# Exponentials in one piece, priorities for the weights' splits and the last scan, and gate tiles per group, in a Mamba-2 plus differential attention trunk

## The chip, the cores and the metric

The kernel runs on one core of a Trainium2 chip. The metric is the device time of one launch in microseconds (us); for several runs the median is given. The engines are named as in the profile: PE is TensorE (matrix products and transposes), PEld its loading of weights, DVE is VectorE, ACT is ScalarE, POOL is GpSimd, SP is SyncE, which issues the DMA transfers here.

## The reference, cut to what matters

One sequence of 512 tokens with 1024 features passes two layers and a last RMSNorm, all in float32.

```
mamba2_layer:  h = rms_norm(x);  z, xbc, dt = split(h @ w_in)
               xbc = silu(causal_conv4(xbc));  xs, B, C = split(xbc)
               per group g (8), heads r (4), head dim 64, state 128:
                 acs   = cumsum(a * dt)                      # inside a chunk
                 y     = (C B^T * exp(acs_l - acs_s), causal) @ (xs*dt)
                       + (C @ state) * exp(acs)
                 state = state*exp(acs_end) + B^T (xs*dt*exp(acs_end - acs))
               y = group_rms_norm((y + d_skip*xs) * silu(z));  x = x + y @ w_out
shared_kv:     k, v = split(rms_norm(x) @ w_kv)
diff_attention_layer: two softmax maps per head on k, weights A1 - lambda*A2, @ v,
               per-head norm, silu gate;  x = x + (...) @ w_out
out = rms_norm(x)
```

The change touches only the first layer: the decays `exp(acs_l - acs_s)`, the gate `silu(z)`, the preparation of the weights, and the order in which the last group's scan is worked.

## The kernel before, in words

**Products in two parts.** Each large product is computed from operands that are split in a high and a low part of a reduced float32 format: `a*b` becomes `ah*bh + ah*bl + al*bh`, three matmuls (`mm3`). A weight segment of 128x2048 is loaded into a `raw` tile (two buffers) by one DMA of SP, then **split** in four (later eight) pieces: `head` makes the high part `whi` on ACT (a scaled copy), `rest` the low part `wlo` on DVE (`raw*gain - whi`). `whi` and `wlo` have two buffers each, so a segment's split waits until the segment two before it has been used by TensorE. `load` (line 122) issues the DMA and gives back the pieces, `lay` (169) writes a piece's two instructions, `fetch` (174) does both for all segments up to a number, and `use` (179) calls it for the next two segments whenever a segment is taken.

**The first layer.** Its work is two streams. The dense one, `stream_a` (521), is all products with weights, in the order `z0 g0 g1 z1 g2 g3 z2 g4 o0 g5 z3 g6 g7 o1 o2 o3`: `z` projects the gates of two groups (four tiles of 128 tokens by 512, PSUM tiles `pz`), `g` projects one group's B, C and x (PSUM tiles `pg`, then the convolution on DVE and ACT), and `o` is the out-projection of two groups (PSUM tiles `po`, added into `x_tok` on DVE). Each `z`, `g` and `o` takes two segments. All of them share four PSUM banks ("mm"). The other stream is `ssd(g)` (552), the scan of a group. It works through C B^T (`pcb`), transposes of B and x (`pbt`, `pxt`), the product with the decays on DVE (`dec` times `pcb`), the states (`psA`, `psB`, `hst`), the output inside the chunk (`pyd`) and from the state (`po` from `hst`), the gate (`u` times `zt`, line 626), the group norm (squares on ACT, the root on DVE, the scaled copy `tmp` on ACT), and the transposes `pyt`, of which `yh` and `yl` are made for the out-projection. The scans use three PSUM banks of their own ("ss") and mostly one SBUF buffer for each kind of tile. The text of the program asks for a group's scan as soon as the group's projection is written.

**Decays.** `decays(j)` (532) prepares two groups. For each it loads the cumulated logarithms, spread over all partitions (a 1 MB DMA into `dec`, two buffers), copies the chunk ends into `een` on POOL, subtracts the tokens' own value and masks, head by head, on POOL. Then for each group ACT takes the exponential of `een` (128x8) and of `dec` in two halves of 128x1024. `een` scales the states in the scan (lines 590 and 594). It is called at the beginning for groups 0 and 1 and within the scan of each odd group for the next two.

**Gates.** `z_out` (344) takes Silu of a 128x512 tile of `pz` on ACT into a `zs` tile (six buffers). Such a tile holds both groups of a pair; it comes free when the later one's scan has used it.

**What sets the order.** Up to line 687 the program is only a list with dependencies. When it is compiled, a scheduler plays it on a model of the engines: among the instructions of an engine that are ready at that moment of the play it takes the one of the highest priority, which is the place in the text where nothing else is said, and gives out the tiles' buffers in the same order. What comes out is a fixed order for each engine; on the chip each engine works through its own list, and an instruction that has to wait holds all behind it on that engine. From line 687 on the order of DVE, ACT and TensorE is that of the text, with the splits placed by hand (`paced`, `use_b`). The loads of ACT's function tables are put in after the scheduling, wherever the next function needs another table.

## Time and profile before

| | |
|---|---|
| median of 3 runs | 737.57 us (736.57 to 738.35) |
| the profiled execution | 736.51 us |
| its span, first to last instruction | 734.7 us |
| granted TensorE clock, mean | 0.998 |
| DMA | 70.83 MB, mean 96 GB/s |

A row of a timeline gives the start in the span, the duration, the engine, the line, the operation, the tile written and the tiles read, the size, and the number of instructions merged in the row; in brackets stands how long the engine had been idle before it and what released it. A row of the waits gives who waited for whom, the sum in us, how often, and the longest. A row of the groups gives the count, the busy time, the mean of one in ns, and the idle time before. Most rows bear line 53, since a helper there records the operations of DVE, ACT and PE; they are told apart by their tiles. A matmul's record is longer than the time after which the next one starts.

### The profile page before, as it was taken

Reading aid. Unit: us, or ns where it says so; the run is one execution under the profiler, and the core shown is the slowest. Engines: PE = TensorE matmul, PEld = TensorE weight load, DVE = VectorE, ACT = ScalarE, POOL = GpSimd, SP = SyncE. Lnnn points to the kernel's source line nnn. Section 1 sums busy time; section 2 is a strip of 40 time slices with the busy share of each in tenths; the row PEclk is TensorE's granted clock in tenths of the full one; section 3 lists DMA queues with packets and bytes.
Section 4 is the critical chain, followed back from the end, with each engine's and each line's share of the span. In section 5 each row is a group of like instructions: output and inputs, shape, how many; then the busy total and the mean of one; then the engine's idle time right before and its main releaser. Section 6 shows DMA issues by size and latency. Waiting matters only on the chain.

```text
span 734.7 us, 10327 instructions
## 1 busy us (share of the span) xinstructions
PE 723.1 (98%) x3733; PEld 605.0 (82%) x3733; DVE 530.8 (72%) x1202; ACT 445.3 (61%) x975; POOL 114.8 (16%) x158
## 2 busy tenths in 40 slices
PE   9999999999999999999999999999999999999996
PEld 7788878888887888877888879888898898889874
DVE  5679955798568669469895655666757857785886
ACT  6849672864829356256433258766766766766566
POOL 0117231402233141150110201000000000000002
PEclk9999999999999999999999999999999999999999
DMA  8552313224132233132113220331221131122003
GB/s 314 215 193 97 128 45 116 78 95 172 59 114 65 108 115 116 58 116 102 71 58 114 87 86 8 115 115 58 65 109 57 58 116 58 58 80 93 29 1 114
DMA packets 12914, 70.83 MB, mean 96 GB/s; under 512 B 1728, under 2 KB 2496, under 8 KB 5312
## 3 DMA queue, kind: packets, MB, share of 16 engines
q1 hardware_dynamic: 12576, 69.90, 26.5%
q8 instruction: 29, 0.48, 0.3%
q10 hardware_dynamic: 288, 0.28, 0.1%
q14 instruction: 21, 0.17, 0.1%
HBM read 68.02 MB, written 2.16 MB: 96 GB/s over the span
## 4 chain that ended last, share of the span: by engine, by line
PE 86%; DVE 6%; ACT 5%; issue 1%; DMA 1%; POOL 0%; ACTq 0%; POOLq 0%; SPq 0%
PE pg L53 20%; PE po L53 13%; PE pz L53 10%; PE pt L53 7%; PE pv L53 6%; PE pq L53 6%; PE pk L53 6%; PE pyd L53 4%; PE pb L53 3%; PE sc L53 3%; PE pc L53 2%; DVE wlo L53 2%; ACT L53 1%; PE pyt L53 1%; PE pxt L53 1%
## 5 line engine op out<-in xcount | busy, mean ns | idle before, releaser
L53 DVE SCALAR_TENSOR_TENSOR wlo<-raw,prm,whi 128x512 fp32r<-128x512 f32 (+1 forms) x256 | 151.4, 640 | 49.6 <-ACT whi L53 49.2
L53 ACT ACTIVATE whi<-raw,prm 128x512 fp32r<-128x512 f32 (+1 forms) x256 | 137.1, 609 | 58.5 <-PE pz L53 12.4
L53 PE MATMUL pg<-a_hi,whi 128*128 128x512 f32 x256 | 102.4, 401 | 0.4 <-DVE xc L53 0.4
L53 PE MATMUL pg<-a_hi,wlo 128*128 128x512 f32 x256 | 102.7, 404 | 0.0
L53 PE MATMUL pg<-a_lo,whi 128*128 128x512 f32 x256 | 101.4, 397 | 0.0
L53 DVE SCALAR_TENSOR_TENSOR xc<-pg,prc,xc 128x511 f32<-128x511 f32 (+2 forms) x96 | 70.0, 743 | 4.4 <-ACT xc L53 3.6
L53 PEld LDWEIGHTS pg<-a_hi,whi 128*128 128x128 f32 x256 | 48.2, 188 | 11.4 <-issue 0.8
L53 PEld LDWEIGHTS pg<-a_hi,wlo 128*128 128x128 f32 x256 | 48.1, 188 | 11.0
L53 PEld LDWEIGHTS pg<-a_lo,whi 128*128 128x128 f32 x256 | 48.2, 188 | 10.8
L53 PE MATMUL po<-whi,yh 128*128 128x512 f32 x128 | 50.9, 400 | 0.7 <-ACT yh L53 0.6
L53 PE MATMUL po<-wlo,yh 128*128 128x512 f32 x128 | 50.9, 400 | 0.4 <-DVE wlo L53 0.4
L53 PE MATMUL pz<-wlo,a_hi 128*128 128x512 f32 x128 | 50.5, 401 | 0.0
L53 PE MATMUL pz<-whi,a_lo 128*128 128x512 f32 x128 | 50.1, 399 | 0.0
L53 PE MATMUL po<-whi,yl 128*128 128x512 f32 x128 | 49.9, 396 | 0.0
L53 PE MATMUL pz<-whi,a_hi 128*128 128x512 f32 x128 | 49.6, 400 | 0.0
L53 ACT ACT_TABLE_LOAD x33 | 42.3, 1283 | 9.5 <-DVE xc L53 7.9
L957 POOL TENSOR_TENSOR ot<-ot,fg 128x512 f32<-128x512 f32 x4 | 5.1, 1285 | 257.6 <-PE pc L53 256.4
L53 ACT ACTIVATE s<-s,mx 128x128 f32<-128x128 f32 (+3 forms) x64 | 35.6, 559 | 9.5 <-DVE mx L53 9.3
L580 POOL TENSOR_TENSOR xe<-xdt,tok 128x256 f32<-128x256 f32 x24 | 15.4, 672 | 152.5 <-DVE xdt L53 152.5
L53 DVE CUSTOM_DVE_ANT_0 s<-sc,bias 128x128 f32<-128x128 f32 (+3 forms) x64 | 29.4, 488 | 12.3 <-PE sc L53 11.9
L53 PE MATMUL pv<-whi,b_hi 128*128 128x256 f32 x128 | 36.6, 286 | 0.0
L53 ACT ACTIVATE tmp<-dx 128x256 f32<-128x256 f32 x32 | 13.1, 411 | 38.0 <-DVE dx L53 38.0
(244 smaller groups left out, 1749.1 us busy)
## 6 DMA issues: line engine op xcount, KB each, us to landing
raw<-in_w_in SPq DMA_DIRECT2D x23, 1024.0 KB, 4.9
raw<-in_w_kvqg SPq DMA_DIRECT2D x16, 1024.0 KB, 4.8
dec<-acs_d SPq DMA_DIRECT2D x8, 1024.0 KB, 4.8
raw<-in_w_out SPq DMA_DIRECT2D x8, 1024.0 KB, 4.7
raw<-in_w_bo SPq DMA_DIRECT2D x4, 1024.0 KB, 4.8
x_tok<-in_x SPq DMA_DIRECT2D x4, 512.0 KB, 9.4
out<-ot SPq DMA_DIRECT2D x7, 256.0 KB, 2.4
raw<-in_w_in SPq DMA_DIRECT2D x4, 256.0 KB, 5.4
```

The source lines that it names most:

```text
L53: i = op(*args, **kw)
L580: GP.tensor_tensor(out=xe[:, c], in0=xdt[:, c], in1=toe_tok[:, c, hs].unsqueeze(2).to_broadcast([P, R, HD]), op=ALU.mult)
L957: GP.tensor_tensor(out=o, in0=o, in1=f, op=ALU.mult)
```

## The change

- `decays` is given the groups' numbers; for each group `dec` and `een` are now two parts of one tile of 2056 columns, and one Exp takes the whole tile. The DMA, the copy and POOL's work stay. All exponentials of a pair still come behind both groups' POOL work in the text.
- `fetch` writes the pieces of a split under high priority (the DMA is issued at the normal one). This holds for the segments that `fetch` loads, those of the first layer.
- The last group's scan, `ssd(7)`, is written under high priority.
- `z_out` makes two Silu of 128x256 into tiles of their own (twelve buffers), one for each group.
- The split of the one segment that borrows the buffers of `dec` takes the first 2048 columns of the larger tile.

```
 def fetch(upto):
     while fetched[0] < min(upto, len(segs)):
-        for piece in load(fetched[0])():
-            lay(piece)
+        pieces_ = load(fetched[0])()
+        with tc.high_priority():
+            for piece in pieces_:
+                lay(piece)
...
 def z_out(j, t, ps):
-    zs = bp2.tile([P, 512], F32, tag="zs", name=f"zs{j}_{t}", bufs=6)
-    A.activation(zs, ps, AF.Silu, scale=r_col[:, t:t + 1])
-    zt[j, t] = zs
+    for i in range(2):
+        zs = bp2.tile([P, 256], F32, tag="zs", name=f"zs{j}_{t}_{i}", bufs=12)
+        A.activation(zs, ps[:, i * 256:(i + 1) * 256], AF.Silu, scale=r_col[:, t:t + 1])
+        zt[2 * j + i, t] = zs
...
-def decays(j):
-    for g in (2 * j, 2 * j + 1):
+def decays(gs):
+    for g in gs:
         hs = slice(R * g, R * g + R)
-        dec = bp.tile([P, R, NQ, P], F32, tag="dec", name=f"dec{g}", bufs=2)
+        both = bp.tile([P, N_DEC], F32, tag="dec", name=f"dec{g}", bufs=2)
+        dec = both[:, 0:R * NQ * P].rearrange("p (h c l) -> p h c l", h=R, c=NQ)
+        een = both[:, R * NQ * P:].rearrange("p (h q) -> p h q", h=R)
...
-        een = small.tile([P, R, 2], F32, tag="een", name=f"een{g}")
         GP.tensor_copy(een, dec[:, :, 1:3, P - 1])
...
-    for g in (2 * j, 2 * j + 1):
-        dec, een = decs[g]
-        A.activation(een, een, AF.Exp)
-        for h in range(0, R, 2):
-            A.activation(dec[:, h:h + 2], dec[:, h:h + 2], AF.Exp)
+    for g in gs:
+        A.activation(decs[g][2], decs[g][2], AF.Exp)
...
-            V.tensor_tensor(out=u[:, c], in0=u[:, c], in1=zt[g // 2, c][:, zo:zo + 256], op=ALU.mult)
+            V.tensor_tensor(out=u[:, c], in0=u[:, c], in1=zt[g, c], op=ALU.mult)
...
-        ssd(g)
+        if g < G - 1:
+            ssd(g)
+        else:
+            with tc.high_priority():
+                ssd(g)
```

## The prediction

> **What bounds the kernel now.** I read the page first, then the list of waits of TensorE, then the timelines around each of those waits. The page's busy table:

> ```profile
> span 734.7 us, 10327 instructions
> PE 723.1 (98%) x3733; PEld 605.0 (82%) x3733; DVE 530.8 (72%) x1202; ACT 445.3 (61%) x975; POOL 114.8 (16%) x158
> ```

> TensorE is busy for 98% of the span; no other engine is near it. A change that touches no matmul, as this one, can gain only what TensorE stands still. The list of TensorE's waits, without the one at the very start and two at the very end, is short:

> ```profile
> PE pyt L53 <- ACT tmp L53: 1.0, 2, 0.7
> PE po L53 <- ACT yh L53: 0.6, 1, 0.6
> PE po L53 <- DVE wlo L53: 0.4, 1, 0.4
> PE pg L53 <- DVE xc L53: 0.4, 1, 0.4
> ```

> All of these lie in the first part (the Mamba layer, up to about 450 us), the only part that the change touches. They add up to 2.4 us of 734.7. The timeline of TensorE shows where they are and what they really cost:

> ```profile
> 227.69 0.71 PE L53 MATMUL po<-whi,yh 128*128 128x512 f32 x2
> 228.82 0.50 PE L53 MATMUL po<-wlo,yh 128*128 128x512 f32 x1 [0.42 <-DVE wlo L53]
> ...
> 236.38 0.40 PE L53 MATMUL po<-wlo,yh 128*128 128x512 f32 x1
> 236.62 0.40 PE L53 MATMUL po<-whi,yl 128*128 128x512 f32 x1
> 237.67 0.44 PE L53 MATMUL pyt<-ident,tmp 128*128 128x128 f32 x2 [0.65 <-ACT tmp L53]
> ...
> 337.50 0.40 PE L53 MATMUL pg<-a_hi,wlo 128*128 128x512 f32 x1
> 338.31 0.47 PE L53 MATMUL pg<-a_hi,whi 128*128 128x512 f32 x1 [0.41 <-DVE xc L53]
> ...
> 428.10 0.39 PE L53 MATMUL po<-whi,yl 128*128 128x512 f32 x1
> 428.88 1.64 PE L53 MATMUL pyt<-ident,tmp 128*128 128x128 f32 x8 [0.39 <-ACT tmp L53]
> 431.08 0.50 PE L53 MATMUL po<-whi,yh 128*128 128x512 f32 x1 [0.57 <-ACT yh L53]
> ```

> A matmul's record lasts 0.40 us, but the next starts 0.24 us after it (236.38 to 236.62), so the printed idle time hides some 0.16 us: a wait costs its printed time and about 0.16 us of refilling. The five are then worth 0.42+0.16 = 0.58 (weights' low part late, 228.8), 0.81 (the scan's output late on ACT, 237.7), 0.57 (a PSUM bank freed late, 338.3), 0.55 and 0.73 (both before and behind the last scan's transposes, 428.9 and 431.1). The sum is **3.24 us, the most that can be won**; below that stands TensorE's own work.

> **The exponential in one instruction.** Now each group has three Exp activations: the small een as soon as it is copied, and two halves of dec. The scheduler places them apart, among Silu activations that need another table. Around the second stall ACT did this:

> ```profile
> 220.03 1.28 ACT L53 ACT_TABLE_LOAD   x1
> 221.32 0.21 ACT L53 ACTIVATE een<-een 128x8 f32<-128x8 f32 x1
> 221.55 1.28 ACT L53 ACT_TABLE_LOAD   x1
> ...
> 224.85 2.56 ACT L53 ACTIVATE whi<-raw,prm 128x512 fp32r<-128x512 f32 x4
> 227.42 1.28 ACT L53 ACT_TABLE_LOAD   x1
> 228.72 1.06 ACT L53 ACTIVATE dec<-dec 128x1024 f32<-128x1024 f32 x1
> 229.80 1.28 ACT L53 ACT_TABLE_LOAD   x1
> ...
> 232.97 1.28 ACT L53 ACT_TABLE_LOAD   x1
> 234.26 1.06 ACT L53 ACTIVATE dec<-dec 128x1024 f32<-128x1024 f32 x1
> ...
> 237.12 1.70 ACT L53 ACTIVATE tmp<-dx,y_y 128x256 f32<-128x256 f32 x4
> ```

> Five loads, 6.4 us, in 14 us, ahead of the tmp that TensorE waited for at 237.67. One exponential per group needs at most one load before and one behind, so three of these five go: 3 x 1.28 = 3.84 us less ACT ahead of tmp, against a wait of 0.65. The een's 0.21 goes too.

> ```profile
> L53 ACT ACT_TABLE_LOAD x33 | 42.3, 1283 | 9.5 <-DVE xc L53 7.9 <-PEq L1112 1.2
> ```

> Over the kernel I expect 20 to 26 loads instead of 33, 9 to 17 us less of ACT's 445. Elsewhere TensorE's list names ACT only at the last scan, so that is worth nothing there. [...]

> Waiting for the whole of dec instead of half costs the scan nothing, since dec is made far ahead of its use. For the last group, the two halves on ACT and the multiplication on DVE:

> ```profile
> 327.28 1.99 ACT L53 ACTIVATE dec<-dec 128x1024 f32<-128x1024 f32 x2
> ```
> ```profile
> 372.88 2.47 DVE L53 TENSOR_TENSOR dec<-dec,pcb 128x512 f32<-128x512 f32 x4
> ```

> The merged instruction takes what the two halves in a row take, at most 1.99 us. From the end of the exponential (329.27) to its use there are 43.6 us of cover; if it were gone, the first half would come about 1 us later. POOL's instructions and the two DMAs of decays stay the same and in the same order. Term: **-0.81 us**.

> **Priority for the weights' splits.** No instruction is added; the four pieces of a split (2.56 us on ACT by the row at 224.85, about as much on DVE) go ahead of older elementwise work. The po matmuls at 227.69 started while their whi had just been made (224.85 to 227.4) and their wlo had not. That segment's whi buffer was last used by the first half of the group projection before; the second half alone is 48 matmuls of 0.24 us, so it was free about 11 us earlier, while ACT was on een and other activations with their loads. With the splits first, that wait goes: **-0.58 us**. For the one at 338.3 the split is one of several things ahead of the convolution that frees the bank; it may come earlier with its split, or be pushed back by the next. Bounds -0.57 to +0.57; I take half of the gain, **-0.29 us**. What is moved past: on ACT and DVE, convolution, gate output and scan of older segments start up to 2.56 us later per split. Splits done earlier free raw earlier, so SP issues the next load earlier. What queues behind a waiting load on SP are the loads of dec, and the wait list of the SP queue says that these wait for their own buffer:

> ```profile
> SPq L537 <- PE pyd L53: 46.9, 6, 10.6
> ```

> Nothing is waiting for them (the cover above): cost nothing.

> **Priority for the last scan.** The last scan's inputs are long there before it is begun. On ACT, the last Silu of its convolution and the first instruction of the scan itself:

> ```profile
> 378.96 0.63 ACT L53 ACTIVATE xc<-xc 128x512 f32<-128x512 f32 x1 [0.67 <-DVE xc L53]
> ...
> 393.57 0.49 ACT L53 COPY bt<-pbt 128x384 f32<-128x384 f32 x1
> ```

> Between them lie 14 us, in which TensorE did out-projections that are also there to be done later. The scan then has to end only 0.55 + 0.73 us earlier to close both stalls. I count the whole: **-1.28 us**. If only a tenth of the 14 us is won, that still holds. Moved behind: the out-projection's adds and splits, which nothing but the same stretch of matmuls waits for.

> **Gates' output in halves.** 16 activations of 128x512 become 32 of 128x256:

> ```profile
> L53 ACT ACTIVATE zs<-pz,ar_col 128x512 f32<-128x512 f32 x16 | 10.6, 678 | 1.4 <-PE pz L53 1.3
> ```

> A scaled copy of 128x256 takes 1.70/4 = 0.43 us (the row at 237.12), so 32 x 0.43 = 13.6, 3.0 us more on ACT, where it is 39% idle. In return half of the buffers come free one group sooner, and with them the PSUM banks that hold pz. TensorE has no wait on pz in its list: gain nothing, cost nothing, 0 to 0.18 us (2 x 0.43 - 0.68) per bank release if the cover goes.

> **The sum.** -0.81 -0.58 -0.29 -1.28 = -2.96 us. Against it stands that every priority reorders the whole schedule on five engines, and a new schedule has its own waits. One new wait of the size of the old (0.55 to 0.81) is the least that I would expect: +0.7. Net -2.3 us. The profiled execution took 736.51 us (its span 734.7 and 1.8 around it), so it becomes 734.2; the median of the runs shown is 737.57, 1.1 above it, and becomes **735.3**. The likeliest case's own range is 734.3 (all of the 3.24) to 736.3.

> **The rivals.**

> *The waits move.* Each of the old waits is replaced by one as long somewhere else. For: the five stalls have four different causes, which looks like the scatter of a greedy schedule and not like a cause to be removed. Against: two of them have a clear cause each. The same result has "the priorities change little": the -0.81 stays alone. Time 736.5 to 738.0.

> *The splits take the scans' place.* A split placed first holds ACT and DVE while the scan's chain (gate product, square, root, scaled copy, transposes) stands behind it, and ACT in program order also waits at the whi until TensorE is done with the buffer. Place: the pyt transposes of groups 0 to 6. For: at 237.67 TensorE already waited for exactly this chain, and the whi pieces were in front of it. Against: TensorE has other matmuls to do then, and the schedule is made with the priorities known. Price: up to 2.56 us for each scan hit. It decides from 2.96/2.56 = 1.2 full hits; with two of them the time is 737.57 - 2.96 + 5.12 = 739.7.

> *The undivided exponential blocks ACT.* An urgent activation that falls behind it waits up to 1.06 us longer than behind a half; eight times that is 8.5 us at worst, 743 us with the rest of the gain. Against: eight coincidences are needed, and the loads saved pay for each. [...]

> **How the numbers follow.** A difference under about 0.2%, 1.5 us, can't be told from none here. The forecast gets 0.58 (of it 0.08 ends within 1.5 us), the waits move 0.22 (0.18 within, 0.02 on each side), the splits take the scans' place 0.17 (0.01 within), the blocking exponential 0.03. Faster 0.50 + 0.02 = 0.52, same 0.08 + 0.18 + 0.01 = 0.27, slower 0.02 + 0.16 + 0.03 = 0.21. The range reaches from 733.4 (all 3.24 won, and 0.9 for the spread of the runs shown, 736.57 to 738.35) to 739.8 (two scans hit).

> **What would show it.** In the profile after: 20 to 26 table loads, eight exponentials of 128x2056 of just under 2 us; no TensorE wait on wlo or on the last scan's tmp and yh, and the first bt of the last scan close behind its convolution; TensorE's waits in the list under 1 us. Wrong it would be with new rows there on tmp, xc or dx in groups 0 to 6, with ACT waiting longer before whi, or with TensorE's last scan still met by po matmuls that ran out.

## The result, and the profile after

The changed kernel took 741.57 us (median of 6 runs, 739.08 to 743.88); the kernel before, run beside it, 737.17 (6 runs, 736.57 to 738.35). The ratio is 1.0055, with a 95% interval of 1.0039 to 1.0071: slower by 4.4 us, where 735.3 was forecast. The profiled execution took 741.79 us.

The page of the changed kernel, busy table:

```profile
span 739.8 us, 10321 instructions
PE 723.0 (98%) x3733; PEld 605.8 (82%) x3733; DVE 536.7 (73%) x1202; ACT 433.8 (59%) x965; POOL 114.5 (15%) x158
```

TensorE's work is the same to 0.1 us and ScalarE is relieved by 11.5, but the span is 5.1 us longer. The list of TensorE's waits of the changed kernel (who waits for whom, sum, times, longest), again without the start and the end:

```profile
PE pg L55 <- DVE y_c L55: 2.0, 1, 2.0
...
PE pbt L55 <- ACT xc L55: 1.2, 1, 1.2
PE pxt L55 <- ACT xc L55: 1.2, 1, 1.2
PE pyt L55 <- ACT tmp L55: 1.0, 1, 1.0
PE pg L55 <- ACT whi L55: 0.9, 1, 0.9
PE po L55 <- DVE x_tok L55: 0.7, 1, 0.7
PE po L55 <- ACT yh L55: 0.6, 1, 0.6
```

They add up to 7.6 us, against 2.4 before: 5.2 more, where the two profiled spans differ by 5.1. Of the five old waits those for `wlo` and for the middle `tmp` are gone; a wait for a PSUM bank (the first row) stands at another place and is five times as long, and the first of the last scan's two grew from 0.39 to 0.99. On TensorE's timeline of the changed kernel:

```profile
67.61 0.66 PE L55 MATMUL pxt<-ident,xc 128*128 128x128 f32 x4 [1.21 <-ACT xc L55]
...
144.03 0.47 PE L55 MATMUL pg<-a_hi,whi 128*128 128x512 f32 x1 [1.98 <-DVE y_c L55]
...
201.20 0.50 PE L55 MATMUL pg<-a_hi,whi 128*128 128x512 f32 x1 [0.94 <-ACT whi L55]
...
238.35 0.50 PE L55 MATMUL po<-whi,yh 128*128 128x512 f32 x1 [0.67 <-DVE x_tok L55]
...
345.18 0.55 PE L55 MATMUL pbt<-ident,xc 128*128 128x128 f32 x3 [1.24 <-ACT xc L55]
...
434.33 1.64 PE L55 MATMUL pyt<-ident,tmp 128*128 128x128 f32 x8 [0.99 <-ACT tmp L55]
436.53 0.50 PE L55 MATMUL po<-whi,yh 128*128 128x512 f32 x1 [0.57 <-ACT yh L55]
```

From here on a new wait is named by its length and the moment at which it begins (the 1.98 at 142 is the one that ends with the row at 144.03); the old ones keep the names that the prediction gave them, by the row that ends them.

The parts themselves came out much as costed. The groups of the changed kernel:

```profile
L55 ACT ACT_TABLE_LOAD x23 | 29.5, 1283 | 5.0 <-DVE xc L55 3.4 <-PEq L1124 1.2
...
L55 ACT ACTIVATE dec<-dec 128x2056 f32<-128x2056 f32 x8 | 15.4, 1923 | 3.2 <-POOL dec L554 3.1
L55 ACT ACTIVATE zs<-pz,ar_col 128x256 f32<-128x256 f32 x32 | 13.1, 472 | 3.5 <-PE pz L55 3.4
```

23 loads (20 to 26 forecast), exponentials of 1.92 us (just under 2), gates 2.5 us dearer on ScalarE (3.0). So what went wrong lies in when things happen, not in what they cost.

### The profile page after: what moved, and what is told of

The parts are those of the page before. It is cut to its first block, busy times and chain, and to the rows that moved or that the text cites. A ratio compares the mean times of both kernels' runs of the same rounds, so it can differ in the third digit from the quotient of the medians.

```text
span 739.8 us, 10321 instructions
## 1 busy us (share of the span) xinstructions
PE 723.0 (98%) x3733; PEld 605.8 (82%) x3733; DVE 536.7 (73%) x1202; ACT 433.8 (59%) x965; POOL 114.5 (15%) x158
## 4 chain that ended last, share of the span: by engine, by line
PE 83%; DVE 10%; ACT 3%; issue 1%; DMA 1%; POOL 0%; ACTq 0%; POOLq 0%; SPq 0%
PE pg L55 18%; PE po L55 13%; PE pz L55 9%; PE pt L55 7%; PE pq L55 6%; PE pv L55 6%; PE pk L55 6%; PE pyd L55 4%; PE pb L55 3%; DVE wlo L55 3%; PE sc L55 3%; DVE xc L55 2%; PE pc L55 2%; DVE y_c L55 1%; PE pxt L55 1%
## 5 line engine op out<-in xcount | busy, mean ns | idle before, releaser
L55 PE MATMUL pg<-a_lo,whi 128*128 128x512 f32 x256 | 103.6, 405 | 0.0
L55 ACT ACTIVATE xc<-pg,prc 128x512 f32<-128x512 f32 x32 | 24.7, 771 | 26.6 <-DVE pg L55 26.2
```

The costliest lines, as they stand in the source:

```text
L55: i = op(*args, **kw)
```

## The experiments

**The parts alone.** First question: which part costs it. The expectations weigh three theories: (1) the gates' halves rewrite the order of the engines' fixed lists, (2) the undivided exponential blocks ScalarE, (3) the splits' priority brings them beside GpSimd's work. Gates' halves alone (the other three parts as before):

> Only the gates' halves; one exponential per part as before, no priorities. Theory 1 (the gates' halves, which the prediction costed at nothing, rewrite the order of the whole first layer and bring the new waits): 740 to 743 us, waits of TensorE 5 us or more in the list. Theory 2 (the merged exponential blocks ACT): 736.5 to 738, like before. Theory 3 (the splits' priority collides with POOL): 736.5 to 738.

Measured: 744.45 us, ratio 1.0097 (1.0081 to 1.0113): worse than the whole change, and above the range of theory 1. Three new waits, 1.60 at 114.3, 1.65 at 175.3 and 2.06 at 239.8, at three different tiles. The exponential alone:

> Only the exponential in one piece; gates and priorities as before. Theory 1: 735 to 738 us, fewer table loads, the wait at the scan's tmp near 237 gone. Theory 2: 739.5 to 742, with TensorE waits behind an ACT that stands at the exponential. Theory 3: as theory 1.

Measured: 736.64, ratio 0.9991 (0.9982 to 1.0000), 23 loads. The wait at 237.7 is gone, but one of 1.34 stands at 336.8 (a bank held by a convolution). Theory 2 is out. Both priorities alone:

> Only the two priorities; exponentials and gates as before. The order of the engines differs from before in few places. Theory 1 and 2: 736 to 738 us, not to be told from before. Theory 3: 739.5 to 742, with wlo pieces over 1 us beside POOL's subtraction.

Measured: 739.15, ratio 1.0025 (1.0015 to 1.0035), between the ranges of the theories. TensorE's timeline of this kernel shows both waits that the splits' priority should have closed, unchanged (0.42 and 0.41 before):

```profile
231.28 0.50 PE L55 MATMUL po<-wlo,yh 128*128 128x512 f32 x1 [0.41 <-DVE wlo L55]
...
340.76 0.47 PE L55 MATMUL pg<-a_hi,whi 128*128 128x512 f32 x1 [0.39 <-DVE xc L55]
```

Compared row by row in the traces (operation, tiles and size, buffer numbers left out), the lists of this kernel differ from before by 18 rows on TensorE, 16 on DVE and 5 on ACT. On DVE and ACT no split of the first layer is among them; what changes places with splits is the end of the last scan, told below. So the splits' priority does hardly anything here. Everything but the gates:

> The whole change without the gates' halves (tiles of 512 columns, six buffers, one activation). Theory 1: 734.5 to 738 us. Theory 2 or 3: 740 to 743.

Measured: 738.04, ratio 1.0010 (1.0000 to 1.0020); waits 1.33 at 337.7, and 1.38 and 0.57 at the last scan. That is at the upper end of what theory 1 expected.

**Is it the halves, or the deal?** With the gates' halves alone, at least 177 rows of TensorE's list, 101 of DVE's and 52 of ACT's stand elsewhere than before (43, 12 and 6 with the exponential alone, halved or merged instructions not counted). So a second theory: every edit gives the scheduler's play another course and so deals the lists anew, whichever edit it is. Three variants of them and one edit that has nothing to do with them, each against before:

```
 e5: two activations of 256 columns into the old 512-column tile, all 16
 e6: the same, but only for the first z         (if j == 0)
 e7: the same, but only for the other three     (if j > 0)
 e8: nothing but   for i in range(24): T.transpose(warm ...)   ->  range(20)
```

(The 24 transposes stand at the very start, ahead of the first product with weights: 1.47 to 5.85 us in the kernel before, the first `pz` at 5.72.)

> Before, with each gate output made by two activations of 128x256 into the old 128x512 tile: the extra instructions without the separate tiles, buffers come free as before. Theory A (any edit that shifts the play re-deals the order, and before was a lucky deal): somewhere from 738 to 745 us, no pattern. Theory B (the buffers that come free earlier are what harms): 736.5 to 738, like before. Theory C (the extra ACT instructions harm by themselves): 743 to 746, as with the separate tiles (744.5).

Measured: 747.07, ratio 1.0129 (1.0113 to 1.0144).

> As the run with halves in one tile, but only for the first z (4 of 16 outputs). Theory A: 738 to 745 us although only four small instructions are added. Theory B: 736.5 to 738. Theory C: a quarter of the loss, 738.5 to 739.5.

Measured: 747.88, ratio 1.0139 (1.0124 to 1.0155). Four more instructions, 10 us; one wait of 6.17 at 236.5.

> Halves in one tile for the other three z (12 of 16 outputs). Theory A: anywhere from 737 to 745 us. Theory B: 736.5 to 738. Theory C: three quarters of the loss, 741.5 to 743.5.

Measured: 735.49, ratio 0.9973 (0.9964 to 0.9983): twelve of the sixteen halved, and faster than before. Its list of waits in the first layer:

```profile
PE po L55 <- DVE xc L55: 0.6, 1, 0.6
PE po L55 <- ACT yh L55: 0.6, 1, 0.6
...
PE pxt L55 <- ACT xc L55: 0.3, 1, 0.3
PE pyt L55 <- ACT tmp L55: 0.3, 1, 0.3
```

> Before, with 20 instead of 24 idle transposes at the start, before any data has come: no part of the change, and no work that the result needs. The fixed order of the engines comes out different. Theory A: 738 to 745 us, by new TensorE waits scattered over the first layer. Theory B and C: 736.5 to 738, like before.

Measured: 749.62, ratio 1.0156 (1.0141 to 1.0171). Four idle transposes less cost 12 us, more than any part of the change; at least 170 rows of TensorE's list, 88 of DVE's and 46 of ACT's differ. Its waits:

```profile
PE po L55 <- DVE x_tok L55: 6.2, 1, 6.2
PE pxt L55 <- ACT xc L55: 2.4, 2, 2.1
```

Theory B (buffers that come free earlier) and theory C (the extra instructions) are out: the old tiles don't help (e5), and a quarter of the extra instructions costs more than all of them while three quarters cost nothing (e6, e7). Theory A has the kind right and the size too small: its ranges were 738 to 745, or 737 to 745 for e7, and all four times lie outside them, on both sides.

The control is 28 transposes, a shift that leaves DVE's list as it was and ACT's and TensorE's nearly (1 row and 12 rows, besides the four transposes):

> The kernel before with 28 instead of 24 of the idle transposes at the very start that wait for the weights; all else as before. The play gives DVE the same order, ACT an order with 5 lines moved, TensorE the same but for the four transposes and 22 lines. Theory (the order of the queues sets the waits, the edit itself nothing): within 1.5 us of before, 736 to 739; TensorE's waits before 450 us again 2.4 to 3.5 us. Rival (four transposes more or less change the start on the chip, and the 12 us of the kernel with 20 come from that): 745 or more.

Measured: 737.24, ratio 0.9999 (0.9989 to 1.0010). Nearly the same lists, same time. And the whole change on 20 transposes (the second of the two runs below) takes 738.63, so 20 of them are not slow in themselves: the 12 us are the other lists, not the four transposes. Two more draws. The better halves with the exponential in one:

> The gates' output in two halves for all but the first z, and the exponential in one instruction; no priorities. If effects of parts add up, -1.8 (halves of the later z) and -0.6 (merge) give 735. If each edit deals anew, as this theory says, the sum means nothing: any time from 735 to 747, and most likely above 736, with 23 to 26 table loads either way.

Measured: 738.50, ratio 1.0016 (1.0007 to 1.0025). -1.9 and -0.6 made +1.2: the effects don't add. And the whole change on 20 transposes:

> All four parts of the change, with 20 instead of 24 idle transposes. Without the change the kernel with 20 took 749.6. Theory (each order is a new draw; the parts themselves are worth 1 us or less): the change's effect at this shift is not the +4 of the kernel with 24; it has another size and probably the other sign, a time of 738 to 748. Rival (the parts themselves cost 4 us): about 754, 4 above 749.6.

Measured: 738.63, ratio to before 1.0019 (1.0009 to 1.0029). With 24 transposes the change costs 4.4 us, with 20 it saves 11.0 (749.62 to 738.63). The 4.4 is not a price of the four parts; it is the difference of two lists.

**The last scan.** Its waits are 0.39 and 0.57 before, 0.34 and 0.57 with the exponential or the gates alone, but 1.37 and 0.57, 1.38 and 0.57, 1.38 and 0.57, 0.99 and 0.57 in the four kernels in which it has priority (e3, e4, e12, the whole change). ScalarE ahead of its `tmp`, before:

```profile
423.06 0.90 ACT L53 ACTIVATE whi<-raw,prm 128x256 fp32r<-128x256 f32 x2
423.87 0.40 ACT L53 ACTIVATE tmp<-dx 128x256 f32<-128x256 f32 x1
```

and after:

```profile
428.14 2.50 ACT L55 ACTIVATE whi<-raw,prm 128x256 fp32r<-128x256 f32 x6
430.54 0.40 ACT L55 ACTIVATE tmp<-dx 128x256 f32<-128x256 f32 x1
```

Six pieces of the next layer's first split stand ahead of the scan's last square, where it was two: 1.6 us more in the one chain that TensorE waits for. And the scan began hardly closer behind its convolution. ScalarE after, from the convolution's Silu (384 us) on:

```profile
383.39 0.64 ACT L55 ACTIVATE xc<-xc 128x512 f32<-128x512 f32 x1
...
390.88 1.71 ACT L55 ACTIVATE tmp<-dx,y_y 128x256 f32<-128x256 f32 x4 [2.25 <-DVE y_y L55]
397.11 0.48 ACT L55 COPY bt<-pbt 128x384 f32<-128x384 f32 x1 [4.52 <-PE pbt L55]
```

The first `bt` comes 13 us after it (14 before), behind the scan before (the `tmp` at 390.88). The room was larger than that: these transposes read only B, the first of the group's four convolved tiles, and TensorE used B and C for `pcb` at 371.55, 25 us ahead of them. The theory: its first transposes need one of the scans' three PSUM banks, and those are given out in the order of the text, to the scan before first; a priority can't change that. The test puts the `pyt` of group 6 into the dense stream's banks, with the last scan's priority alone:

```
-            pyt = ss_bank(f"pyt{g}_{j}")
+            pyt = (mm_bank if g == G - 2 else ss_bank)(f"pyt{g}_{j}")
```

> Priority for the last scan alone, with the transposes pyt of the scan before it (group 6) put into the four banks of the dense stream instead of the scans' three. Theory (the last scan cannot start early because its first transposes wait in the play for a bank that is given to group 6's pyt first): the last scan's bt begins within 3 us of its convolution's last Silu instead of 14, and TensorE has no wait on the last scan's tmp or yh. Rival (the priority is too weak or the scan too long): bt 10 us or more behind, the two waits stay at about 1 us or more together. The time is left open, 735 to 745, since the order changes in 75 to 100 lines.

Measured: 766.36, ratio 1.0392 (1.0369 to 1.0416). On ScalarE the last scan's first transposes were now copied 5 us before group 6's `tmp`:

```profile
365.48 0.46 ACT L55 COPY bt<-pbt 128x384 f32<-128x384 f32 x1
...
370.42 1.71 ACT L55 ACTIVATE tmp<-dx,y_y 128x256 f32<-128x256 f32 x4 [2.08 <-DVE y_y L55]
```

and no wait is left on the last scan's tmp or yh. So the bank was what held the transposes: with other banks for group 6 they come even ahead of the rest of their own convolution, whose last Silu ran at 403.69. That the two waits went says less, since 140 rows of TensorE's list differ and it waits 6.59, 5.49 and 3.87 us elsewhere; the kernel is 29 us slower, far outside the 735 to 745 expected.

**What makes a list late?** Two candidates. ScalarE's table loads (1.28 us each) are put in after the lists are made, so the play doesn't know of them. And VectorE ran slower beside GpSimd (1.48 us for a low part beside its subtraction, 0.74 just before it, in the rows below). An edit that changes the lists can't tell them apart, so these leave every list as it is (compared row by row in the traces, table loads aside). First the loads: Silu instead of Exp in the decays (other values come out), which leaves out the loads around them. ScalarE is then busy for 221.1 of the first 447 us instead of 239.0.

```
-            A.activation(decs[g][2], decs[g][2], AF.Exp)
+            A.activation(decs[g][2], decs[g][2], AF.Silu)
```

> The changed kernel with Silu instead of Exp in the decays (other values, so the output is wrong; same sizes). Every engine's order is exactly that of the changed kernel; only table loads go, 23 to 7. Theory L (loads that the play does not know of make the new order late): the waits at 200 and 344, whose ACT work stands behind a load and an exponential, go, the one at 66 shrinks: 741.6 - (0.94+0.16) - (1.24+0.16) - 0.6 = 738.5. Theory P (VectorE slowed beside GpSimd makes it late): TensorE's 1.98 at 142 stays, and so does most of the rest: 741 or more.

Measured: 737.84 (737.57 to 741.32). ScalarE after, ahead of the `whi` that TensorE waits for at 200:

```profile
195.54 1.28 ACT L55 ACT_TABLE_LOAD   x1
196.84 1.92 ACT L55 ACTIVATE dec<-dec 128x2056 f32<-128x2056 f32 x1
198.76 1.28 ACT L55 ACT_TABLE_LOAD   x1
200.06 0.47 ACT L55 ACTIVATE zs<-pz,ar_col 128x256 f32<-128x256 f32 x1
200.43 2.55 ACT L55 ACTIVATE whi<-raw,prm 128x512 fp32r<-128x512 f32 x4
```

Without the loads, the waits at 66, 200 and 344 are gone, as theory L of the expectation said, and the one for a bank (now at 141) is left, as theory P said:

```profile
PE pg L55 <- DVE y_c L55: 1.7, 1, 1.7
...
PE pyt L55 <- ACT tmp L55: 1.0, 1, 1.0
PE po L55 <- DVE x_tok L55: 0.9, 1, 0.9
```

The same with the worst of these lists (before on 20 transposes), with before itself as control, and with the gates' halves alone:

> The kernel before with 20 idle transposes (749.6), with Silu instead of Exp in the decays (output wrong, same sizes); the same order, 33 loads become 7. Theory L: the 2.13 at 69.9, which has five loads in the 15 us ahead of it, goes with its refill and its stretch of half clock (2.3 + 1.7): 745.6 or less; if the 6.17 at 238.6 has to do with the load at 231.6 it shrinks by up to 1.3 more. Theory P: the 6.17 stays above 5.

Measured: 744.17 (743.72 to 744.43). The 2.13 at 69.9 went, the 6.17 stayed (6.07).

> The kernel before with Silu instead of Exp in the decays (output wrong, same sizes): the same order on every engine, 33 loads become 7. If the loads cost only where an order runs late, before can gain at most its wait at 237.7 and the one at 338.3 (0.81 + 0.57) plus a tenth or two: 736 to 737.4. If the loads cost each order as much as the changed one (3.7 us there), 733.7.

Measured: 733.96 (733.76 to 734.16), ratio 0.9954 (0.9937 to 0.9971).

> The gates' halves alone (744.45) with Silu instead of Exp in the decays (output wrong, same sizes), at the same order; 31 loads become 9. Its waits: 1.60 at 114.3 (behind yh, with two loads in the 6 us ahead), 1.65 at 175.3 (no load in the 9 us ahead), 2.06 at 239.8 (three or four loads in the 12 us ahead). If the loads make it late, the first and the third go, 4.0 us with refill, and 740.5 is left or less; if not, 743 or more.

Measured: 737.70, ratio 1.0005 (0.9993 to 1.0016). The waits at 114 and 240 went, the 1.65 at 175 stayed.

| lists of | with loads | without | the loads cost |
|---|---|---|---|
| before | 737.12 | 733.96 | 3.2 |
| the change | 741.57 | 737.84 | 3.7 |
| gates' halves alone | 744.45 | 737.70 | 6.8 |
| before, 20 transposes | 749.62 | 744.17 | 5.5 |

(The kernel before, run beside each of them, had medians of 737.1 to 737.4.) Here the control matters. Alone, the 3.7 us of the changed kernel look like nearly the whole of its 4.4. But the loads cost the kernel before 3.2 as well; they explain 0.6 of the 4.4, and 3.9 stay between the two (737.84 to 733.96). For the gates alone they explain 3.6 of 7.3, for the shift 2.3 of 12.5. With means in place of medians (the executions of e13 fall in two groups, see the last section) the loads cost the changed kernel 2.5 us (741.4 to 738.9) and the one before 3.3 (737.3 to 734.0), and explain nothing. Either way, as the main cause of the changed kernel's loss the loads are out.

Then GpSimd. After, VectorE and GpSimd ahead of the 1.98 at 142:

```profile
132.25 0.74 DVE L55 SCALAR_TENSOR_TENSOR wlo<-raw,prm,whi 128x512 fp32r<-128x512 f32 x1
...
133.25 4.45 DVE L55 SCALAR_TENSOR_TENSOR wlo<-raw,prm,whi 128x512 fp32r<-128x512 f32 x3
...
138.67 0.55 DVE L55 TENSOR_SCALAR y_i<-v 128x4 int32<-128x4 int32 x1
...
140.91 0.15 DVE L55 TENSOR_TENSOR y_c<-y_c,y_y 128x4 f32<-128x4 f32 x1
```
```profile
133.13 5.48 POOL L553 TENSOR_TENSOR dec<-dec,tok 128x512 f32<-128x512 f32 x4
138.56 2.39 POOL L554 TENSOR_SCALAR_AFFINE_SELECT dec<-dec 128x512 f32<-128x512 f32 x4
```

The low part just before GpSimd's subtraction took 0.74 us, the three beside it 1.48 each, and the root's first four small steps 0.41 to 0.55 instead of 0.15 (2.05 together). That is 3 x 0.74 + 1.45 = 3.7 us more in the queue ahead of the convolution whose bank TensorE waits for. Two runs, with the lists kept again, do GpSimd's subtraction for 16 of the 128 partitions only (the rest of the decays is left unsubtracted):

```
-  GP.tensor_tensor(out=dec[:, h], in0=dec[:, h], in1=acs_tok[:, :, R*g+h]...to_broadcast([P, NQ, P]), op=ALU.subtract)
+  GP.tensor_tensor(out=dec[0:16, h], in0=dec[0:16, h], in1=acs_tok[0:16, :, R*g+h]...to_broadcast([16, NQ, P]), op=ALU.subtract)
```

> The changed kernel with GpSimd's subtraction done for 16 of the 128 partitions (output wrong); the order of every engine is exactly that of the changed kernel, and the instructions' length along the free axis is the same. If GpSimd slows VectorE by the data that it moves, VectorE's low parts beside it fall from 1.48 to about 0.7 and the 1.98 at 142 goes: 741.6 - 2.1 = 739.5 or less. If it slows it by the time that its instruction lasts, nothing changes: 741 to 742.5. In both, the waits at 200 and 344 stay.

Measured: 742.76 (741.13 to 744.40); the wait at 142 is 2.20, the one at 344 stays and the one at 200 is gone, where TensorE now comes 2 us later. The groups and VectorE's timeline of this kernel:

```profile
L553 POOL TENSOR_TENSOR dec<-dec,tok 16x512 f32<-16x512 f32 x32 | 35.3, 1128 | 0.5
```
```profile
133.45 3.65 DVE L55 SCALAR_TENSOR_TENSOR wlo<-raw,prm,whi 128x512 fp32r<-128x512 f32 x3
...
138.07 0.97 DVE L55 TENSOR_SCALAR y_i<-v 128x4 int32<-128x4 int32 x1
139.08 1.14 DVE L55 TENSOR_SCALAR y_y<-y_i 128x4 int32<-128x4 int32 x1
```

An eighth of the data takes GpSimd as long (1.13 us for each of 32, 1.16 with all partitions), and VectorE is slowed as much: the slowest low parts beside the subtraction take 1.53 us in both kernels (four rows in the changed one, three here and one of 1.59), against 0.76 in the mean of those away from it. That the three at 133 take 3.65 and not 4.45 goes with the later start of the subtraction (133.66 instead of 133.13); the slowing moved on to the root's steps, of which the first, at 0.97, stands beside the subtraction and the second, at 1.14, beside the mask, which still works on all partitions.

> The kernel before with 20 idle transposes (749.6), GpSimd's subtraction for 16 of 128 partitions (output wrong); same order on every engine. VectorE lost about 0.9 + 1.8 + 0.9 us beside GpSimd between 229 and 238: if that goes, the 6.17 at 238.6 becomes about 2.6, and the stretch of half clock behind it (6.8 us, worth 3.4) shrinks or goes: 742.5 to 746. If the slowing goes by time and not by data: 749.6, 6.17 stays.

Measured: 750.73 (749.01 to 750.84); the 6.17 is 6.12. So the slowing didn't go by the number of partitions (1.53 us beside 16 as beside 128). GpSimd's instruction lasted as long in both (1.13 and 1.16 us); that the slowing goes by this time was not shown, since no run shortened the instruction along its free axis. These two runs did not take the slowing away, and so cannot say what it costs. That it makes the wait at 142 is read from the rows, not shown by a run.

## Why the prediction was wrong

**The step that failed: the gates' halves at "gain nothing, cost nothing", and +0.7 for all new waits of a new schedule.** I priced each part where it stands in the old lists, and let the new lists cost "the least that I would expect". In fact the five new waits came to 6.0 us where the sum has +0.7, TensorE's waits grew by 5.2 in all, and the scatter between lists is several times the sum of all terms: 735.5 to 749.6 us over the lists of edits that cost next to nothing in themselves (e6, e7, e8). The whole change is +4.4 on one start and -11.0 on another (e12), so neither number belongs to its parts. That the halves' extra ScalarE time hides is not refuted (+2.5 us of ACT, and e7 with most of it is faster), but they are the part that changes the lists most, and alone they bring +7. The rival "the waits move" named the right kind ("the scatter of a greedy schedule") and put its price at the size of the old waits. The old waits, 2.4 us in all, are those of a good draw; they don't measure what a draw can cost.

Where the 3.9 us lie that the loads don't explain: TensorE's waits without loads are, after against before, 1.74 against none (at 141), 0.86 against 0.20 (at 235), 1.00 against 0.34 (last scan), 0.40 against none (at 17), and 0.24 against 0.40 near 340. That is 3.3 us, 3.6 with the refill of two waits more. Half of it is the wait behind VectorE and GpSimd at work side by side (why it is late is argued above, not shown), a fifth is the last scan's priority.

**The exponential, -0.81: right in kind.** Loads, duration and the end of the wait at 237.7 came as worked out; alone it measured -0.6, with a new wait of 1.34 beside it. The rival in which an undivided exponential blocks ACT came true at two of eight places in the changed kernel: at 200, ahead of `whi`, and at 66, where ScalarE itself waited 2.38 us for GpSimd's mask before it; ahead of the wait at 344 one stands too, with other work and a load in between. All three waits need the loads as well (e13). Its 743 us lies nearest to the measured time, but by luck: alone, the exponential in one costs nothing (e2). Whether one instruction or several is the better way is not decided by these runs: merging alone gave -0.6, halving the gates -1.9 to +10.5, by which ones were halved.

**The splits' priority, -0.58 and -0.29: wrong.** Both waits stay with it (e3). I took a late split for one that was passed over; its priority moves almost no row, so in the play, it seems, there was nearly nothing older and ready to pass. In the changed kernel the wait for `wlo` is gone, but with other lists. The rival "the splits take the scans' place" gave 739.7, nearer than the forecast, but not by its mechanism, since the priority that it needs does next to nothing.

**The last scan, -1.28: wrong in sign, +0.6 in the changed kernel.** I saw 14 us of room and no reason against; the reason was the bank's owner. I also counted only out-projections among what a priority would pass, and not that the next layer's split would fall in front of the scan's end.

**"3.24 us, the most that can be won": not a bound.** The kernel before without loads won 3.2 while waits of 0.40, 0.34 and 0.56 stayed. The list of waits of PEld, where a weight load waits under the record of the matmul before, shows what the list of PE hides. Before:

```profile
PEld pyt L53 <- ACT tmp L53: 4.4, 13, 1.1
```

and without loads:

```profile
PEld pyt L55 <- ACT tmp L55: 1.8, 6, 0.8
```

Thirteen times transposes waited, of which TensorE's own list names two. Since the two kernels have the same lists, their rows can be laid side by side: the eight transposes at 105.02, where TensorE's list names no wait, take 1.74 us before and 1.04 without loads, and all that follows them starts 0.9 us earlier. The prediction's sum uses none of that list.

What stays open: why the 6.17 of e6 and e8 arises (the loads give 0.1 of it in e8; no run took the slowing beside GpSimd away), and whether any rule foretells a good list. The best kernel found is e7, 735.49; nothing makes its list better than a lucky one.

## What to carry to other kernels

Where a scheduler plays the program and fixes every engine's list, an edit's own cost is only a part of its price; compare it under a few neutral shifts (some idle instructions more or less at the start) before believing a difference of 1 or 2%. To ask what a resource costs, change it so that the lists stay row for row the same, and do the same to the kernel before: without that control the table loads would have passed for the cause. A priority only helps an instruction that is ready and passed over; look first at who holds its buffer or bank.

## What the runs showed of the hardware

```profile
144.00:148.00 4.00, 3.97 (x17) 3.28 (x18) 2.99 (x7) 3.97 (x5) 0.00 (x0) 1.00 0.01 2
```
```profile
144.00:148.00 4.00, 3.56 (x9) 2.88 (x10) 3.08 (x8) 3.97 (x5) 0.00 (x0) 0.60 0.01 2
```

The clock was 0.5 for 3.4 us at that wait, and at those of 2.13 (e8) and 3.87 (e5); for 6.8 us at 6.17 (e6, e8) and at a 3.87 in e11, and for 10.2 at 5.49 and 6.59 there. In these traces every wait of 2.13 us or more has such a stretch, and at those of 5.49 and more it begins inside the wait. From 2.06 us down it is mixed: 1.98 and 2.06 (the changed kernel, e1) brought none, 1.65 brought 3.4 us in e18 and none in e1, 1.37 or 1.38 with 0.57 close behind brought 3.4 in e3 and e12 (mean granted clock 0.995 in both) and none in e4 (0.999). What such a stretch costs beyond the wait can be read where the lists are the same: across 3.4 us of it TensorE's rows fall back by 1.5 us in e15 against the changed kernel, and by 1.6 in e18 against e1. One kernel can have it in some executions and not in others. Of the ten of e13, six took 737.6 to 737.9 us at a mean granted clock of 0.997 to 0.999, four 740.0 to 741.3 at 0.992 to 0.995; 3.4 us at half clock lower such a mean by 0.002 (3.4 x 0.5 / 738). The slow stretches lasted one to three times 3.4 us, and a wait of 2.13 us, and once of 1.65, was enough for one; why 1.98 and 2.06 had none was not shown.

**GpSimd's price didn't fall with its partitions.** VectorE's low parts beside a GpSimd subtraction of 16 partitions took 1.53 us, as beside one of 128, against 0.76 in the mean of those away from it. In the trace VectorE's instructions are lengthened and not waiting: the three low parts at 133.25 in the changed kernel take 4.45 us in a row, with no idle time between them. What in the two engines makes them longer was not shown.
